# Layer 1 of a two-layer diffusion trunk on Trainium2: 64 of 256 tokens moved from the dense expert products to gathered rows

## Chip, cores and metric

One core of one Trainium2 chip runs the whole program. The metric is device time in microseconds; lower is better. Most executions of a kernel agree within 0.3%.

## What is computed

Two layers over 256 latent and 256 context tokens of width 1024; each is a mixer (attention) and an expert network (PEER) of 16384 experts. Layer 0 needs all 512 tokens, layer 1 only the 256 latents. For each token and each of 8 heads the network takes the best 16 of 16384 experts by product keys, and weights their rows:

```python
q = (xb @ wq).reshape(PEER_TBLOCK, PEER_HEADS, 2, PEER_DQ // 2)
s = jnp.einsum('thpd,pnd->thpn', q, sub_keys).astype(jnp.float32)
sv, si = lax.top_k(s, PEER_TOPK)
...
fv, fp = lax.top_k(cand, PEER_TOPK)
eidx = jnp.take_along_axis(cidx, fp, axis=-1)
g = jax.nn.softmax(fv, axis=-1)
ue = jnp.take(u, eidx, axis=0)
ve = jnp.take(v, eidx, axis=0)
a = jnp.einsum('thkd,td->thk', ue, xb).astype(jnp.float32)
wgt = (jax.nn.gelu(a, approximate=False) * g).astype(xb.dtype)
return jnp.einsum('thk,thkd->td', wgt, ve)
```

So a token has 128 slots (8 heads x 16), each with one row of u and one of v.

## The kernel before, in words

The engines: PE multiplies, ACT casts and evaluates functions, DVE works on elements, POOL (GpSimd) issues gathers, SP issues the other transfers. A float32 matrix is split into a high part, rounded by ACT's cast to the product type (L167), and a low rest that DVE subtracts (L168); a product is then three (L191 to L193: high by high, high by low, low by high). Some products are made in whole float32 instead (L213).

`peer(l, xs, sq, nd)` is the expert network of layer l, with `nd` token blocks of 128 done densely: layer 0 calls it with 3 of 4 blocks, layer 1 with 2 of 2. A dense block multiplies with all 16384 experts, in 128 chunks of 128. For chunk i, `achunk(i)` computes u times the tokens: 24 products (8 parts of the width, three each) whose moving operand has as many columns as there are dense tokens, 384 in layer 0 and 256 in layer 1. ACT applies Gelu into a ring of tiles (L1023). `weight(i)` multiplies the tile with the gate matrix (L1151, zero where the expert is not chosen), and splits it into the tile `w2` (L1152 ACT, L1153 DVE). `split_v(i)` splits v's rows into two `vs` tiles, and `fchunk(i)` multiplies: per dense block two halves of 512 columns, three products each, summed in PSUM over all chunks.

The gate matrix G is built before the loop. `prologue` routes each block (`route`), then `gates` makes 16 groups of 8 tokens per block: DVE and ACT write one-hot operands, PE multiplies them (L954), ACT copies out (L957), and SP writes the stage tile to G in DRAM, read back in the loop as tiles `g` of four chunks, in two buffers (L1139). In the same stretch the first `lag` = 47 calls of `achunk` of layer 1 run, every fifth in whole float32. The main loop then runs j from 0 to 127: load v(j+2), `achunk(j + 47)` while there is one (81 times), `split_v(j+1)`, `weight(j+1)`, `fchunk(j)`. There are four `vs` tiles (two chunks) and two `w2` tiles.

The fourth block of layer 0 goes by gathered rows: its tokens lie on the 128 partitions, and for each of 128 slots POOL issues an indirect DMA of 128 rows of 4 KB into one of five `gr` buffers (L1111), after copying its indices to a small tile (L1105, L1108) whose first copy waits for a `w2` tile and so keeps the pace. DVE multiplies a u row with the token and sums it (L1118); after all u slots, Gelu and gates, it adds each v row with its weight to `acc` (L1123). Layer 1 has none of this.

The order on each engine is set by a scheduler in the language's framework, which moves instructions away from the order in which the code writes them.

Of the kernel before, what the change touches and what calls it, by code (L numbers as in the profile page):

```python
# [10 lines left out]
F = mybir.dt.float32  # L11
# [58 lines left out]
GAT = {"gr": 5, "hn": 1, "ga": 1, "idx": 1, "ix": 3}  # L70
# [5 lines left out]
class Phase:  # L76
    """a pool whose tags have a set number of buffers"""
# [13 lines left out]
class Kernel:  # L91
# [103 lines left out]
    def proj_t(self, key, hh, hl, c=512, **kw):  # L195
        """[128 columns, c tokens] in PSUM"""
# [35 lines left out]
    def ada_mm(self, l, v, half, pool):  # L232
        """half of one modulation vector for both conditions, in rows 0 and 1 of each 32 as four partial sums"""
# [142 lines left out]
    def rope(self, x, p, perm, cos, sin, n):  # L376
        """x [128, n] from p in PSUM, its first 256 columns (the latents) rotated, the rotation after the next one"""
# [59 lines left out]
    def probs1(self, P, S, scale, sink=None, bias=None):  # L437
        """P [128, 2, nk] <- exp of the two heads' scores less their maximum; sums in sm"""
# [31 lines left out]
    def flip(self, x, nk, eng):  # L470
        """[128, 128 nk] -> [128 keys, nk, 128]"""
# [113 lines left out]
    def mixer1(self, xs, sq):  # L585
# [10 lines left out]
        # cq | ckv in natural layout  # L596
# [38 lines left out]
        # kr (replicated), dq, dk transposed  # L635
# [17 lines left out]
        # latent queries, keys and values  # L653
# [124 lines left out]
    def top16(self, V, X, a, b):  # L778
        """sorted top 16 of each a, b as scratch, interleaved over the lists"""
# [12 lines left out]
    def route_scores(self, l, T, nd, hh, hl):  # L792
        """sorted top 16 of each half key for the dense blocks; scores of a further block go to DRAM"""
# [44 lines left out]
    def route(self, sv, al):  # L838
        """experts i, j and gates of one token block; a generator, leaves them in self.rt"""
# [63 lines left out]

    def gates(self, go, ti, G):
        """gate matrix of 128 tokens -> DRAM; a generator"""
# [58 lines left out]
        for n in range(16 + GPIPE):  # L964
            if n < 16:
# [6 lines left out]
    def peer(self, l, xs, sq, nd):  # L972
        """nd dense token blocks; a further block, if any, goes by gathered rows; returns the pieces of f"""
# [3 lines left out]
        TD = nd * 128  # L977
# [9 lines left out]
        rg = Phase(self.tc, "ring%d" % l, {"ring": lag + 2})  # L987
        self.wn = Phase(self.tc, "win%d" % l, W_BUFS)
        routes, sd = self.route_scores(l, T, nd, hh, hl)
        G = self.dp.tile([32, 128, 4 * nd, 4, 32], F, name="G%d" % l)  # L990
# [34 lines left out]
        # routing and gate matrix, with the first products of the main loop in between  # L1025
        def prologue():
            for _ in routes[0]:
                yield RW
            for t in range(nd):
                nxt = routes[t + 1] if t + 1 < nd else None  # L1030
                for n, _ in enumerate(self.gates(self.rt[t], t, G)):
# [3 lines left out]
                if nxt:  # L1035
                    for _ in nxt:
                        yield RW

# [8 lines left out]
        tot = (6 * nd - EARLY[l]) * RW + nd * (32 + 2 * GPIPE)  # L1047
# [14 lines left out]
        mn = Phase(self.tc, "main%d" % l, {**MAIN, **(GAT if T > nd else {})})  # L1062
        acc = None
        if T > nd:
            acc = self.const([128, 1024], name="acc")
            nc.vector.memset(acc, 0.0)
            ga = mn.t("ga", [128, 2, 128])
            idx = mn.t("idx", [128, 128], I32)
            hn = mn.t("hn", [128, 1024])
            for half in range(2):  # L1070
                p = self.ps([128, 4, 128])
                for k in range(4):
                    tt = slice(TD, TD + 128)
                    nc.tensor.matmul(p[:, k, :], hh[:, half * 4 + k, tt], self.identr, start=True, stop=False)
                    nc.tensor.matmul(p[:, k, :], hl[:, half * 4 + k, tt], self.identr, start=False, stop=True)
                nc.scalar.copy(hn[:, half * 512:half * 512 + 512], p.rearrange("p a b -> p (a b)"))
# [21 lines left out]
        def gather(n0, n1, after=None):  # L1098
            """rows of slots n0..n1, not before after is there"""
            n1 = min(n1, 256)  # L1100
# [5 lines left out]
            for a, b in ((n0, min(n1, 128)), (max(n0, 128), n1)):  # L1106
                if a < b:
                    nc.gpsimd.tensor_copy(ix[:, a - n0:b - n0], idx[:, a % 128:a % 128 + b - a])  # L1108
# [351 lines left out]
```

## Time and profile before

| | us |
|---|---|
| median of 3 runs | 2739.52 (2731.03 to 2754.28) |
| span of the profiled execution | 2734.2 |
| PE busy in it | 2610.7 (95%) |
| DVE busy | 1876.3 (69%) |
| ACT busy | 1267.3 (46%) |
| POOL busy | 529.2 (19%) |

The span runs from the first to the last instruction of the execution that the profiler recorded; its own time with what lies around the span is not listed, the runs are timed without the profiler. Busy shares are means over all stages, so each stage is to be read by itself. A product's duration is longer than its distance to the next, since products overlap: rates are read from starts. In the groups, the last figures are the idle time of the engine just before, and what ended most of it.

### The profile page before, as it was taken

The numbers are of one execution on the slowest core, as the hardware profiler recorded it, in microseconds if no ns is written. First come the engines' busy times: TensorE is split into PE (matmuls) and PEld (weight loads), VectorE is DVE, ScalarE is ACT, GpSimd is POOL, SyncE is SP. The second block draws the span as 40 slices with busy tenths as digits, with TensorE's granted clock in tenths as the row PEclk, the third lists the DMA queues.
The fourth block names the chain that finished last, engine by engine and source line by source line (L and its number), as shares of the span: only waits on it lengthen the run. The fifth ranks groups of instructions, "written<-read, shape, count | busy, mean of one in ns | idle before, by whom it ended". The sixth has DMA issues, their size and how long they took to land.

```text
span 2734.2 us, 43073 instructions
## 1 busy us (share of the span) xinstructions
PE 2610.7 (95%) x16265; PEld 2261.8 (83%) x16265; DVE 1876.3 (69%) x3862; ACT 1267.3 (46%) x2201; POOL 529.2 (19%) x534
## 2 busy tenths in 40 slices
PE   7999998989999999999999989998999999999998
PEld 6866787878899999999899767757999899999986
DVE  4267588886977777777777765365997565555455
ACT  3255335997333333333333333343499444444454
POOL 0000000000045555566565530000000000000000
PEclk9999999999999999999999998998999999999999
DMA  7262323977688888888888862453467976565355
GB/s 291 101 216 86 111 88 128 287 235 246 232 313 311 308 315 306 316 299 321 294 309 288 275 225 75 164 195 113 144 215 242 318 267 210 208 211 214 130 193 183
DMA packets 240977, 614.15 MB, mean 225 GB/s; under 512 B 18384, under 2 KB 102608, under 8 KB 240768
## 3 DMA queue, kind: packets, MB, share of 16 engines
q1 hardware_dynamic: 203904, 477.17, 50.6%
q0 software_dynamic: 36864, 134.23, 13.9%
q8 instruction: 127, 2.08, 0.3%
q14 instruction: 82, 0.67, 0.1%
HBM read 558.90 MB, written 52.43 MB: 224 GB/s over the span
## 4 chain that ended last, share of the span: by engine, by line
PE 62%; DVE 6%; DMA 3%; ACT 3%; issue 2%; POOL 1%; SPq 0%; DVEq 0%; POOLq 0%; ACTq 0%
PE p L192 19%; PE p L191 19%; PE p L193 19%; DMA gr<-in_v,ix 1%; PE p L213 1%; PE s L707 1%; PE p L229 1%; DVE ws L168 1%; ACT stage L957 1%; ACT og L940 1%; DVE vs L168 1%; DMA sc<-sd 1%; PE p L954 1%; ACT ws L167 1%; PE p L245 0%
## 5 line engine op out<-in xcount | busy, mean ns | idle before, releaser
L167 ACT CAST ws<-w 128x1024 fp32r<-128x1024 f32 (+1 forms) x327 | 343.0, 1050 | 634.0 <-PE p L192 581.4
L168 DVE TENSOR_TENSOR ws<-w,ws 128x1024 fp32r<-128x1024 f32 (+1 forms) x327 | 397.5, 1216 | 267.7 <-ACT ws L167 267.4
L192 PE MATMUL p<-vs,w 128*128 128x512 f32 x1280 | 502.2, 393 | 7.5 <-DVE vs L168 7.5
L167 ACT CAST vs<-v 128x1024 fp32r<-128x1024 f32 x256 | 269.5, 1053 | 509.5 <-PE p L192 509.5
L191 PE MATMUL p<-vs,w 128*128 128x512 f32 x1280 | 499.6, 391 | 4.4 <-ACT vs L167 4.4
L193 PE MATMUL p<-vs,w 128*128 128x512 f32 x1280 | 501.6, 392 | 0.0
L191 PE MATMUL p<-hh,ws 128*128 128x384 f32 (+2 forms) x1336 | 472.2, 354 | 6.2 <-ACT ws L167 2.9
L193 PE MATMUL p<-hh,ws 128*128 128x384 f32 (+2 forms) x1336 | 466.0, 349 | 1.5 <-DVE ws L168 1.5
L192 PE MATMUL p<-hl,ws 128*128 128x384 f32 (+2 forms) x1336 | 466.6, 349 | 0.0
L168 DVE TENSOR_TENSOR vs<-v,vs 128x1024 fp32r<-128x1024 f32 x256 | 312.8, 1222 | 152.7 <-ACT vs L167 151.0
L191 PE MATMUL p<-hp,ws 128*128 128x256 f32 x1032 | 295.5, 287 | 1.8 <-ACT ws L167 1.1
L193 PE MATMUL p<-hp,ws 128*128 128x256 f32 x1032 | 292.8, 284 | 0.8 <-DVE ws L168 0.8
L192 PE MATMUL p<-hp,ws 128*128 128x256 f32 x1032 | 293.2, 284 | 0.0
L192 PEld LDWEIGHTS p<-vs,w 128*128 128x128 f32 x1280 | 241.3, 189 | 56.5 <-DVE vs L168 11.1
L193 PEld LDWEIGHTS p<-vs,w 128*128 128x128 f32 x1280 | 240.9, 188 | 53.7 <-DVE w L1153 3.0
L191 PEld LDWEIGHTS p<-vs,w 128*128 128x128 f32 x1280 | 241.1, 189 | 50.6 <-ACT vs L167 4.6
L191 PEld LDWEIGHTS p<-hh,ws 128*128 128x128 f32 x1336 | 255.0, 191 | 24.7 <-ACT ws L167 4.3
L192 PEld LDWEIGHTS p<-hl,ws 128*128 128x128 f32 x1336 | 254.6, 191 | 14.9 <-issue 0.5
L193 PEld LDWEIGHTS p<-hh,ws 128*128 128x128 f32 x1336 | 254.5, 190 | 13.1 <-DVE ws L168 2.0
L1123 DVE SCALAR_TENSOR_TENSOR acc<-gr,ga,acc 128x1024 f32<-128x1024 f32 x128 | 164.2, 1283 | 102.3 <-DMA gr<-in_v,ix 101.7
L1118 DVE SCALAR_TENSOR_TENSOR gr<-gr,hn 128x1024 f32<-128x1024 f32 x128 | 156.2, 1224 | 108.5 <-DMA gr<-in_u,ix 102.5
L311 POOL TENSOR_TENSOR rso<-rsm,mhalf 128x1 f32<-128x1 f32 x30 | 20.1, 671 | 1079.4 <-DVE rsm L309 1079.4
(267 smaller groups left out, 4127.6 us busy)
## 6 DMA issues: line engine op xcount, KB each, us to landing
w<-in_uT SPq DMA_DIRECT2D x256, 512.0 KB
v<-in_v SPq DMA_DIRECT2D x256, 512.0 KB
w<-in_ada_w SPq DMA_DIRECT2D x96, 512.0 KB
G<-stage SPq DMA_DIRECT2D x40, 1024.0 KB
g<-G SPq DMA_DIRECT2D x32, 768.0 KB
w<-in_wq SPq DMA_DIRECT2D x32, 512.0 KB
g<-G SPq DMA_DIRECT2D x32, 512.0 KB
w<-in_w_out SPq DMA_DIRECT2D x16, 512.0 KB
```

What stands on the lines that cost most here:

```text
L167: self.nc.scalar.copy(hi, raw)
L168: self.nc.vector.tensor_tensor(lo, raw, hi.bitcast(F), op=OP.subtract)
L191: m(out, lh, rh, start=start, stop=False)
L192: m(out, lh, rl, start=False, stop=False)
L193: m(out, ll, rh, start=False, stop=stop)
L213: self.nc.tensor.matmul(out, w[:, k * 128:(k + 1) * 128], self.h32[:, k, :], start=k == 0, stop=k == 7)
L229: self.nc.tensor.transpose(out, x, self.ck("ident"))
L707: nc.tensor.matmul(S[:, s, :], a[c][h, q], b[c][h, :], start=True, stop=kind == "d", tile_position=(64 * s, 0))
L940: nc.scalar.activation(og_[:, 1, g, :, b], oh[:, 1, g, :, b], AF.Copy, scale=gl[:, k:k + 1])
L954: nc.tensor.matmul(p[:, k, :], oh[:, 0, g, :, b], og_[:, w, g, :, b], start=(w == 0), stop=(w == 1))
L1118: nc.vector.scalar_tensor_tensor(t, t, 1.0, hn, op0=OP.mult, op1=OP.mult, accum_out=ga[:, 0, n:n + 1])
L1123: nc.vector.scalar_tensor_tensor(acc, t, ga[:, 0, n - 128:n - 127], acc, op0=OP.mult, op1=OP.add)
```

## The change

Layer 1 calls `peer(1, xs, sq, 1, 1)`: one dense block of 128 tokens, and the second block is split. Its first 64 tokens stay dense, but their weights' high and low parts lie side by side as one operand of 128 columns, so that two products (with v high, v low) take the place of three; the sum of the two halves of the result is taken at the end by a product with a matrix `fold`. Its other 64 tokens go by gathered rows: each token lies on two partitions, 64 slots on each (`spread` moves the indices and gates there), so that there are 64 gathers of u rows and 64 of v rows, spread over the loop from its first iteration, with six buffers. The u products have 192 columns, the gate tiles 192 tokens, and the gate groups are 16 + 8 in place of 32. The low part of the 64 packed tokens is subtracted on POOL. u and v become one tensor per layer.

```diff
-GAT = {"gr": 5, "hn": 1, "ga": 1, "idx": 1, "ix": 3}
+GAT = {0: {"gr": 5, "hn": 1, "ga": 1, "idx": 1, "ix": 3}, 1: {"gr": 6, "hn": 1, "ix": 3, "pk": 2}}
...
-            self.nc.tensor.matmul(out, w[:, k * 128:(k + 1) * 128], self.h32[:, k, :], start=k == 0, stop=k == 7)
+            self.nc.tensor.matmul(out, w[:, k * 128:(k + 1) * 128], self.h32[:, k, :out.shape[-1]], start=k == 0, stop=k == 7)
...
-        TD = nd * 128
+        GT = 64 if packed else 128
+        GS = 128 * GT // 128
+        TD = T * 128 - GT
+        NP = TD // 32
+        DD = nd * 128
...
-                for n, _ in enumerate(self.gates(self.rt[t], t, G)):
+                if t == nd:
+                    spread(self.rt[t])
+                for n, _ in enumerate(self.gates(self.rt[t], t, G, 16 if t < nd else 8)):
...
+            ii = self.wn.t("rt", [128, 128], I32, name="ii")
+            nc.vector.scalar_tensor_tensor(ii, go[:, 0, :], 128.0, go[:, 1, :], op0=OP.mult, op1=OP.add)
+            for s in range(2):
+                nc.sync.dma_start(idx[64 * s:64 * s + 64, :], ii[64:128, 64 * s:64 * s + 64])
+                nc.sync.dma_start(ga[64 * s:64 * s + 64, 1, :], go[64:128, 2, 64 * s:64 * s + 64])
...
+        if packed:
+            hd = mn.t("gr", [128, 8, 2, GT], name="hd")
+            for s in range(2):
+                nc.gpsimd.tensor_copy(hd[:, :, s, :], self.h32[:, :, tt])
...
+                if packed:
+                    self.transpose(p[:, k, :], hd[:, kk].rearrange("p s t -> p (s t)"))
...
-            nc.scalar.copy(w[:, 0, :], wl)
-            nc.vector.tensor_tensor(w[:, 1, :], wl, w[:, 0, :].bitcast(F), op=OP.subtract)
+            nc.scalar.copy(w[:, :TD], wl)
+            h = w[:, :TD].bitcast(F)
+            if packed:
+                nc.gpsimd.tensor_tensor(w[:, TD:TD + GT], wl[:, DD:], h[:, DD:], op=OP.subtract)
+            nc.vector.tensor_tensor(w[:, 2 * TD - DD:], wl[:, :DD], h[:, :DD], op=OP.subtract)
...
+            if packed:
                 for half in range(2):
                     for i, vh, vl, w in ops:
                         b = slice(half * 512, half * 512 + 512)
-                        self.mm3(fps[t][half], w[:, 0, tt], w[:, 1, tt], vh[:, b], vl[:, b], i == 0, i == NCH - 1)
+                        for m, v in enumerate((vh, vl)):
+                            nc.tensor.matmul(fps[nd][half], w[:, DD:DD + 128], v[:, b], start=i == 0 and m == 0,
+                                             stop=i == NCH - 1 and m == 1)
...
-        NGB = 5
-        lt = late() if T > nd else None
+        NGB = GAT[l]["gr"]
+        first = 0 if packed else LATE
+        lt = None if packed else late()
...
+                pk = mn.t("pk", [128, 512])
+                nc.scalar.copy(pk, fps[nd][half])
+                p = self.ps()
+                for s, x in enumerate((pk, acc[:, half * 512:half * 512 + 512])):
+                    nc.tensor.matmul(p[64 * s:64 * s + 64, :], self.fold, x, start=True, stop=True,
+                                     tile_position=(0, 64 * s))
```

The new lines keep their places a little further down: L168 of before is L169, L1151 is L1181, L1153 is L1186, L1118 is L1148, L1111 is L1141; POOL's subtraction is L1185.

The scheduler gives DVE another order where layer 1's main loop begins. Before, from the splits of the first two chunks of v (vs) to those of the third and the fourth (ws is a split of u, ring<-ring,g the multiply with the gates, w the low part of the weights):

```order
L168 TENSOR_TENSOR vs<-v,vs 128x1024 x2
L1151 TENSOR_TENSOR ring<-ring,g 128x256
L168 TENSOR_TENSOR ws<-w,ws 128x1024
L1151 TENSOR_TENSOR ring<-ring,g 128x256 x2
L168 TENSOR_TENSOR vs<-v,vs 128x1024
L1153 TENSOR_TENSOR w_20847<-ring,w_20847 128x256
```

Now, from the same two splits to that of the third chunk (gr,ga<-gr,hn is the use of a gathered u row):

```order
L169 TENSOR_TENSOR vs<-v,vs 128x1024 x2
L169 TENSOR_TENSOR ws<-w,ws 128x1024
L1181 TENSOR_TENSOR ring<-ring,g 128x192 x4
L169 TENSOR_TENSOR ws<-w,ws 128x1024
L1181 TENSOR_TENSOR ring<-ring,g 128x192 x16
L169 TENSOR_TENSOR ws<-w,ws 128x1024
L1181 TENSOR_TENSOR ring<-ring,g 128x192
L1148 SCALAR_TENSOR_TENSOR gr,ga<-gr,hn 128x1024 x7
L169 TENSOR_TENSOR ws<-w,ws 128x1024
L1148 SCALAR_TENSOR_TENSOR gr,ga<-gr,hn 128x1024
L169 TENSOR_TENSOR vs<-v,vs 128x1024
L1186 TENSOR_TENSOR w_20659<-ring,w_20659 128x128
```

Between the second and the third split of v stood four instructions; now there stand 33: 21 multiplies with the gates of later chunks, four splits of u and eight uses of gathered rows.

POOL had nothing of layer 1's main loop; the row before the end of its list, the factors of the norms, is all that stood there. Now it has this as the loop begins (hd is the copy of the 64 tokens, ix the index tile):

```order
L1096 COPY hd<-h_17511 128x8x64 x2
L1138 COPY ix<-idx 128x6
L1141 DMA gr<-in_u,ix 128x1024 x2
L1185 TENSOR_TENSOR w_20538<-ring,w_20538 128x64
L1141 DMA gr<-in_u,ix 128x1024 x3
L1185 TENSOR_TENSOR w_20596<-ring,w_20596 128x64
L1135 COPY ix<-w_20596 128x1
L1138 COPY ix<-idx 128x2
L1141 DMA gr<-in_u,ix 128x1024 x3
L1185 TENSOR_TENSOR w_20659<-ring,w_20659 128x64
```

Each chunk's subtraction now stands in one list with the index copies and the gathers.

## Rows read from the trace of the kernel before

**Rows 1.** The page's head: the span of the profiled execution.

```profile
span 2734.2 us, 43073 instructions
```

**Rows 2.** Windows (us, each engine's busy us and count, PE clock, DMA share, GB/s).

```profile
736.00:1173.00 437.00, 436.49 (x2205) 396.77 (x2205) 329.57 (x482) 150.84 (x208) 227.25 (x224) 1.00 0.87 311
1950.00:2117.60 167.60, 161.46 (x1462) 154.72 (x1461) 144.62 (x343) 146.06 (x278) 0.00 (x0) 0.99 0.67 211
2117.60:2139.90 22.30, 17.89 (x138) 17.27 (x136) 8.99 (x12) 12.16 (x20) 0.00 (x0) 1.00 1.01 340
2139.90:2591.00 451.10, 451.10 (x2879) 411.38 (x2880) 264.14 (x364) 213.67 (x319) 0.00 (x0) 1.00 0.62 219
2591.00:2718.80 127.80, 127.80 (x567) 105.54 (x566) 72.05 (x93) 62.81 (x93) 0.00 (x0) 1.00 0.57 197
...
2132.00:2144.00 12.00, 7.59 (x41) 6.52 (x40) 7.17 (x12) 5.07 (x8) 0.00 (x0) 0.86 0.98 380
```

**Rows 3.** Timeline of PE in layer 1's loop (start us, us, engine, line, op).

```profile
2301.71 0.28 PE L191 MATMUL p<-hp,ws 128*128 128x256 f32 x1
...
2304.58 0.40 PE L191 MATMUL p<-vs,w 128*128 128x512 f32 x1
...
2307.33 0.28 PE L191 MATMUL p<-hp,ws 128*128 128x256 f32 x1
```

**Rows 4.** Timeline of PE and its weight loads (PEld), layer 0.

```profile
662.05 0.22 PE L1074 MATMUL p<-identr,hh 128*128 128x128 f32 x1
...
662.10 0.28 PE L1075 MATMUL p<-identr,hl 128*128 128x128 f32 x1
662.16 0.19 PEld L1074 LDWEIGHTS p<-identr,hh 128*128 128x128 f32 x1
662.22 0.27 PE L1074 MATMUL p<-identr,hh 128*128 128x128 f32 x1
```

**Rows 5.** Timeline of PE before layer 1's loop.

```profile
2083.18 3.67 PE L213 MATMUL p<-h,w 128*128 128x256 f32 x16
2086.69 2.00 PE L954 MATMUL p<-og,oh 128*128 128x128 f16 x32
2088.73 0.39 PE L191 MATMUL p<-hp,ws 128*128 128x256 f32 x1
```

**Rows 6.** The page's groups: DVE on gathered rows (count, busy us, mean ns, idle).

```profile
L1123 DVE SCALAR_TENSOR_TENSOR acc<-gr,ga,acc 128x1024 f32<-128x1024 f32 x128 | 164.2, 1283 | 102.3 <-DMA gr<-in_v,ix 101.7
L1118 DVE SCALAR_TENSOR_TENSOR gr<-gr,hn 128x1024 f32<-128x1024 f32 x128 | 156.2, 1224 | 108.5 <-DMA gr<-in_u,ix 102.5
```

**Rows 7.** Groups of POOL; last, one line's durations (ns min/median/max).

```profile
L1111 POOL DMA_INDIRECT gr<-in_v,ix x128 | 177.1, 1383 | 45.1 <-POOL ix L1108 22.5 <-issue 21.1 <-DVE ws L168 0.9
...
L1108 POOL COPY ix<-idx 128x3 int32<-128x3 int32 (+3 forms) x111 | 88.3, 796 | 188.1 <-DVE idx L1091 181.5
L1105 POOL COPY ix<-w 128x1 f32<-128x1 f32 x109 | 65.6, 602 | 277.2 <-ACT w L1152 276.4 <-issue 0.3
...
L1105 POOL COPY ix<-w x109: 181/473/2787, 766.0 to 1594.6; 128x1 f32<-128x1 f32 x109
```

**Rows 8.** Timeline of DVE, then of POOL, in layer 0's loop.

```profile
916.06 1.22 DVE L168 TENSOR_TENSOR ws<-w,ws 128x1024 fp32r<-128x1024 f32 x1
...
916.24 1.09 POOL L1108 COPY ix<-idx 128x3 int32<-128x3 int32 x1
```

**Rows 9.** Timeline of DVE and PE as layer 1's loop begins ([idle before <-releaser]).

```profile
2136.49 1.09 DVE L1151 TENSOR_TENSOR ring<-ring,g 128x256 f32<-128x256 f32 x3 [7.98 <-DMA g<-G]
...
2139.90 1.91 PE L191 MATMUL p<-vs,w 128*128 128x512 f32 x4 [4.41 <-ACT vs L167]
```

**Rows 10.** Timeline of ACT, DVE and PE in the loop's tail.

```profile
2651.04 1.05 ACT L167 CAST vs<-v 128x1024 fp32r<-128x1024 f32 x1 [1.36 <-PE p L192]
...
2652.13 1.22 DVE L168 TENSOR_TENSOR vs<-v,vs 128x1024 fp32r<-128x1024 f32 x1 [1.16 <-ACT vs L167]
...
2653.79 0.39 PE L191 MATMUL p<-vs,w 128*128 128x512 f32 x1
```

More of the change, by code (lines that the diff above doesn't have):

```diff
@@ L962, in product @@
                                       stage[:, 64 * c:64 * c + 64, :].rearrange("p (c i) t -> p c (i t)", i=4))
-        for n in range(16 + GPIPE):
-            if n < 16:
+        for n in range(blocks + GPIPE):
+            if n < blocks:
                 build(n)
@@ L970, in gates, with peer @@
             yield
-    def peer(self, l, xs, sq, nd):
+    def peer(self, l, xs, sq, nd, packed):
         nc = self.nc
@@ L986, in peer @@
         self.m.close()
-        rg = Phase(self.tc, "ring%d" % l, {"ring": lag + 2})
+        rg = Phase(self.tc, "ring%d" % l, {"ring": lag + 2, **GIDX[l]})
         self.wn = Phase(self.tc, "win%d" % l, W_BUFS)
-        routes, sd = self.route_scores(l, T, nd, hh, hl)
-        G = self.dp.tile([32, 128, 4 * nd, 4, 32], F, name="G%d" % l)
+        routes, sd = self.route_scores(l, T, nd + packed, hh, hl)
+        G = self.dp.tile([32, 128, NP, 4, 32], F, name="G%d" % l)
         self.rt = []
@@ L1028, in prologue @@
                 yield RW
-            for t in range(nd):
-                nxt = routes[t + 1] if t + 1 < nd else None
-                for n, _ in enumerate(self.gates(self.rt[t], t, G)):
+            for t in range(nd + packed):
+                nxt = routes[t + 1] if t + 1 < nd + packed else None
+                if t == nd:
+                    spread(self.rt[t])
+                for n, _ in enumerate(self.gates(self.rt[t], t, G, 16 if t < nd else 8)):
                     yield 1
@@ L1046, in peer @@
         i = 0
[L1047 removed]
+        tot = (6 * (nd + packed) - EARLY[l]) * RW + nd * (32 + 2 * GPIPE) + packed * (16 + 2 * GPIPE)
         done = 0
@@ L1061, in peer @@
         self.wn.close()
[L1062 to L1076, printed above, removed]
+        mn = Phase(self.tc, "main%d" % l, {**MAIN, **GAT[l]})
+        if self.acc is None:
+            self.acc = self.const([128, 1024], name="acc")
+        acc = self.acc
+        nc.vector.memset(acc, 0.0)
+        if not packed:
+            ga = mn.t("ga", [128, 2, GS])
+            idx = mn.t("idx", [128, GS], I32)
+        hn = mn.t("hn", [128, 1024])
+        tt = slice(TD, TD + GT)
+        if packed:
+            hd = mn.t("gr", [128, 8, 2, GT], name="hd")
+            for s in range(2):
+                nc.gpsimd.tensor_copy(hd[:, :, s, :], self.h32[:, :, tt])
+        for half in range(2):
+            p = self.ps([128, 4, 128])
+            for k in range(4):
+                kk = half * 4 + k
+                if packed:
+                    self.transpose(p[:, k, :], hd[:, kk].rearrange("p s t -> p (s t)"))
+                else:
+                    nc.tensor.matmul(p[:, k, :], hh[:, kk, tt], self.identr, start=True, stop=False)
+                    nc.tensor.matmul(p[:, k, :], hl[:, kk, tt], self.identr, start=False, stop=True)
+            nc.scalar.copy(hn[:, half * 512:half * 512 + 512], p.rearrange("p a b -> p (a b)"))
         def late():
@@ L1181, in peer @@
         weight(0)
+        if packed:
+            gather(0, NGB)
         for j in range(NCH):
@@ L1198, in peer @@
         fchunk([NCH - 2, NCH - 1])
+        if not packed:
+            f = [[acc[:, 0:512], acc[:, 512:1024]]]
+        else:
+            f = []
+            for half in range(2):
+                pk = mn.t("pk", [128, 512])
[4 more added lines that the diff above has]
+                                     tile_position=(0, 64 * s))
+                f.append(p)
+            f = [f]
         mn.close()
         rg.close()
-        return [fps[t] if t < nd else [acc[:, 0:512], acc[:, 512:1024]] for t in range(T)]
+        return fps[:nd] + f
     def residual(self, l, f):
@@ L1264, in run @@
         nc.vector.tensor_copy(self.io2, self.ck("iota")[:, :, None].to_broadcast([128, 128, 2]))
+        self.acc = None
+        self.fold = self.const([128, 64], name="fold")
+        nc.vector.tensor_tensor(self.fold, self.ck("ident")[:, 0:64], self.ck("ident")[:, 64:128], op=OP.add)
         self.identr = self.const([128, 128], R, name="identr")
@@ L1438, in layout @@
     z["uT"] = peer_u.reshape(2, 128, 128, 8, 128).transpose(0, 1, 4, 3, 2)
-    z["u0"] = peer_u[0]
-    z["v"] = peer_v
+    for l in range(2):
+        z["u%d" % l], z["v%d" % l] = peer_u[l], peer_v[l]
     z["fg"] = final_norm_g
```

47 lines of the change are left out of this document (28 added, 19 removed).

## Prediction

> **What bounds the kernel now.** I read the windows first, one row per stage, then the timeline inside a stage for who waits for whom, then the groups by line for durations. Of the 2734.2 us [rows 1] the change reaches the expert block of layer 1. In it TensorE (PE) is busy nearly all the time: 161.5 of 167.6 us from the routing to the last gate product, 17.9 of 22.3 us in the change over to the main loop, 451.1 of 451.1 and 127.8 of 127.8 us in the loop [rows 2]. So the loop is a string of PE products. While u products remain, an iteration costs 24 of them with 256 columns in 2304.58 - 2301.71 = 2.87 us (0.120 each) and 12 v products with 512 columns in 2307.33 - 2304.58 = 2.75 us (0.228 each): 5.62 us [rows 3]. The last 48 iterations are v products alone, 12 x 0.228 = 2.72 us. As a check, 80 x 5.62 + 48 x 2.72 = 580 us, and from the first F at 2139.9 [rows 9] to 2718.8 PE is full in each row of rows 2, 578.9 us. VectorE (DVE) has slack there (264 of 451 us) and GpSimd (POOL) does nothing at all [rows 2].
>
> **The change part by part.** I write A for the 24 u products of a chunk and F for its v products.
>
> *F: 12 products become 10* (six for the dense block, four for high and low side by side): 10 x 0.228 = 2.28 us, 0.45 us less.
>
> *A: 256 columns become 192.* No row has 192. From 0.228 at 512 and 0.120 at 256 the slope is 0.42 ns a column, which gives 0.093. But with 128 columns the products of [rows 4] follow each other at 0.11 (662.10 to 662.22, with a weight load that begins between them at 662.16), while the first pair, whose loads were taken during the wide product before, was 0.05 apart (662.05 to 662.10) [rows 4]. So I read the load as a floor of 0.11, and a narrow product as not slower by itself. I take 0.111: A is 2.66 us, 0.22 less; ends 0.093 and 0.120. "TensorE: Matmul & The Clock Gate" of the Trainium skill, section LDWEIGHTS, says the same against this change: a load takes its columns over 1.2 GHz, estimated at 107 ns, whatever the product's width; by streaming alone A would be 2.23 us and the loop some 35 us shorter than I say.
>
> So on PE alone an iteration would be 4.93 us, then 2.28 us. Whether it gets there hangs on four covers.
>
> *DVE.* It gains 64 u rows (1.22 us) and 64 v rows (1.28 us) [rows 6], 128 uses over 206 half iterations: 1.24 per full iteration, 0.62 in a tail one. Its multiply shrinks from 0.36 (1.09 for three, [rows 9]) to about 0.28 and its subtraction to 0.21. A full iteration has 2 x 1.15 for the splits (1.22 us in rows 8; I take off the overlap of one instruction with the next, which the three multiplies of rows 9 show too), 0.28, 0.21 and 1.24 x 1.18: 4.25 us of 4.93. It fits, with 14% to spare.
>
> *POOL* is new in this loop: a subtraction of 64 columns per chunk, two small index copies and the gathers' descriptors. A gather takes 1.38 plus 0.35 of idle (45.1 us over 128) [rows 7]; 1.24 of them are 2.1 us, the copies 0.60 and 0.80: 3.5 us without the subtraction. No row has that. Its bounds are the shortest and the longest copy of one element, 0.2 and 2.8 [rows 7]. A three element copy lasted 1.09 us because DVE's split, begun 0.18 before it, ended 1.04 after it [rows 8]; so I take 0.35 for the work and 0.65 for the wait, 1.0: 4.5 us of 4.93. The Trainium skill's "SBUF — State Buffer", section "SBUF: two separate sides", has the rule: the port pair of DVE and GpSimd is an exclusive lock, and who starts first holds it for the whole instruction. Rows 8 agree, with 1.09 us. By the rule at its full price every subtraction waits out a whole split, 1.55 in all, and the sum below would be -3; with no lock at all the tail would run at PE's 2.28 and the sum would be -58.
>
> *DMA.* A full iteration loads u and v (0.524 MB each), a quarter of the gate tile (0.098) and 1.24 x 0.524 of gathered rows: 1.80 MB. At 4.93 us that is 365 GB/s. The loop of layer 0 had 311 at a DMA share of 0.87 with PE full, and the change over 380 at 0.98 [rows 2]. So it is just below what was seen, with queueing. With these three near 90% I give a full iteration 5.10 us: 80 x (5.62 - 5.10) = 42 us less; ends 4.93 (55 less) and 5.78 (1.80 MB at 311; 13 more).
>
> *The tail.* Here two buffers of vs and w2 make a chain: ACT's vs cast starts as F(j-1) ends (2651.04), DVE's split follows (2652.13 for 1.22), F(j+1) starts at 2653.79 [rows 10], about 2.75 us after the cast. Today this is in time by some 0.4 us. With F at 2.28 it is not: the packed products come first and need POOL's low part, and POOL must wait until that split ends, 2.3 us after the cast, then 0.35. Period 2.7; in the 62% of iterations with a gather POOL is late by another 0.5 to 1. I take 3.0: 48 x (3.0 - 2.72) = 13 us more; ends 2.28 (21 less) and 3.9 (57 more, POOL's subtraction at 2.0).
>
> *Before the loop.* 33 split A chunks at 24 x 0.009 = 7.1 us; 9 chunks in whole float32 whose 16 products take 0.219 (3.51 / 16, [rows 5]) and in proportion 0.165: 7.6 us; 8 gate groups of 16 products at 0.064 (2.04 / 32): 8.2 us. Together 22.9; with PE at 161.5 of 167.6 I take 20; ends 15 and 23. The last five chunks gain nothing: from the last gate product to the first F PE waits anyway for G to be written and read back (DVE idle 7.98 for it, PE 4.41, [rows 9]), and the copies, transposes and hn lie in that wait. Cost 0; if the copies are late, 3.
>
> *The order at the loop's start* costs. Before, DVE has three multiplies and one ws split between the second and the third vs split. Now it has 21 multiplies, four ws splits and eight uses there: 5.9 + 4.6 + 9.4 = 20 us of work, and the gate tile has two buffers, so each four multiplies wait for a load. PE has F, A, F, A to do meanwhile, 9.9 us. So PE waits 10 us for DVE's work alone; with some 2 us for each of four loads 18, with the 14 multiplies and a use before the next split 22, and with the clock that falls after such a pause (0.86 in the stretch with the 4.41 us pause, [rows 2]) 24. Ends 10 and 32.
>
> *The end.* Four products fold the halves, behind the last F, while DVE works on the first block: 1 us; ends 0 and 3.
>
> Sum: -20 + 24 - 42 + 13 + 1 = -24 us on the profiled 2734.2: 2710. The median of the runs, 2739.5, lies 5.3 above that span (the page gives the span alone, so what lies around it I leave as it is): about 2716.
>
> **Rivals.**
> 1. *The covers hold, PE alone decides.* -20 + 10 - 55 - 21 + 1 = -85: 2655. For it: PE was full in layer 0 beside gathers [rows 2]. Against: three engines at 90%, and the order above.
> 2. *Slower: POOL becomes the bound.* Place: the subtraction between index copies and descriptors. At T us for it an iteration takes 3.5 + T, a tail one 1.9 + T (0.62 of 3.1, plus T). It eats the whole gain from T = 1.6 (tail 3.5, 37 us more instead of 13); at T = 2.0 the sum is -20 + 24 - 10 + 58 + 1 = +53: 2793. For it: copies of one to three elements took 0.6 and 0.8 on average and up to 2.8 [rows 7]. Against: T that high needs a full wait each time, and DVE has gaps.
> 3. *DMA becomes the bound.* At 311 GB/s: +13 in full iterations, 0.95 MB in 3.05 us in the tail +16, -20 + 24 + 1: +34, 2773. For it: no long stretch shows more. Against: 380 over 12 us.
> 4. *The narrow product is dearer*, two passes a column: 0.173, 2870. Against: the 0.05 of [rows 4].
>
> **How the numbers follow.** Forecast 0.52, its own range 2690 to 2745; rival 1 0.22, rival 2 0.13, rival 3 0.08, rival 4 0.05. A difference under 1% (27 us) is about what a measurement of this kernel cannot tell from none. Under 2712 lie rival 1 and 45% of the forecast: 0.45. Over 2767 lie nearly all of rivals 2 and 4 and half of rival 3: 0.21. The rest is 0.34. The range leaves out a tenth below, where all covers hold and the start costs nothing, and a tenth above: 2665 to 2780.
>
> **What would show it.** Starts of u products with 192 columns 0.11 apart; full iterations of 5.0 to 5.2 us and tail ones of 2.7 to 3.2, where PE's waits name POOL's subtraction; one wait of PE of 10 us or more for vs within 30 us of the loop's start; DMA near 350 GB/s. It is wrong if PE waits in the loop for gathers or u loads instead, if the subtraction takes over 1.6 us, or if the start runs through.

## The result, and the profile after

| | before | changed |
|---|---|---|
| median of 4 runs, us | 2739.95 (2731.03 to 2754.28) | 2835.75 (2830.6 to 2847.5) |
| ratio to before (95% interval) | | 1.0345 (1.0317 to 1.0373) |
| span of the profiled execution, us | 2734.2 | 2828.5 |

The changed kernel is slower by 3.45%. The forecast was 2716, with a range from 2665 to 2780. The windows of the changed kernel by stage (columns as in rows 2): routing to the last gate product, the change over to the first F, the first four iterations, the other 76 full ones, the tail, and a piece of the first four.

```profile
1952.00:2107.60 155.60, 141.72 (x1315) 138.83 (x1314) 128.02 (x300) 118.65 (x226) 2.26 (x2) 0.96 0.63 196
2107.60:2135.90 28.30, 19.79 (x149) 19.31 (x146) 10.07 (x16) 13.77 (x23) 8.47 (x11) 0.82 1.02 360
2135.90:2186.30 50.40, 27.12 (x139) 23.38 (x137) 30.95 (x69) 10.31 (x16) 13.66 (x16) 0.70 0.77 265
2186.30:2653.40 467.10, 408.57 (x2586) 361.61 (x2584) 331.43 (x457) 193.74 (x303) 235.56 (x325) 0.95 0.84 287
2653.40:2814.50 161.10, 127.16 (x483) 94.13 (x481) 99.08 (x120) 61.23 (x95) 73.11 (x110) 0.94 0.71 232
2150.00:2170.00 20.00, 10.29 (x36) 8.68 (x37) 17.90 (x35) 1.95 (x3) 10.72 (x10) 0.51 0.67 215
```

Where rows 2 had PE full in every stretch of the loop, it now idles 23 of 50, 59 of 467 and 34 of 161 us. The times by stage, counted between the starts of F products, in us (the last two columns belong to experiments below):

| stage | before | changed | difference | forecast | uses behind | ramp |
|---|---|---|---|---|---|---|
| start of the first F | 2139.9 | 2135.9 | -4.0 | -20 | | |
| first 4 iterations | 24.2 | 50.4 | +26.2 | +22 | 49.3 | 19.9 |
| the other 76 full ones | 427.1 | 467.2 | +40.1 | -40 | 377.0 | 377.0 |
| 48 tail ones | 130.6 | 161.0 | +30.4 | +13 | 134.4 | 132.7 |
| after the last F | 12.4 | 14.0 | +1.6 | +1 | | |

The forecast's 42 for 80 iterations and 24 for the start are shared out here as 40 and 22. The start is as forecast in size; the 76 iterations have the wrong sign. What PE and DVE waited for in these 76 (waits by engine: who for whom, us in total, times, longest):

```profile
PE p L1198 <- DVE vs L169: 55.8, 32, 5.1
PE p L1198 <- POOL w L1185: 2.4, 1, 2.4
...
DVE gr L1148 <- DMA gr<-in_u,ix: 68.0, 32, 6.6
DVE acc L1153 <- DMA gr<-in_v,ix: 65.9, 17, 7.9
```

PE waits for DVE's split of v, DVE waits for gathered rows. DVE is busy 331.4 of these 467.1 us and waits 133.9 for rows, together 465.3: it has hardly any other idle time, so its work and its waits for rows make up the iteration. The timeline shows one such pause, on POOL, DVE, PE, ACT, and then the next gather and its use:

```profile
2235.05 0.97 POOL L1141 DMA_INDIRECT gr<-in_u,ix  x1 [0.27 <-POOL ix L1138]
2236.33 1.90 POOL L1141 DMA_INDIRECT gr<-in_u,ix  x1 [0.30 <-issue]
...
2238.88 1.21 DVE L169 TENSOR_TENSOR vs<-v,vs 128x1024 fp32r<-128x1024 f32 x1
...
2241.43 1.23 DVE L1148 SCALAR_TENSOR_TENSOR gr<-gr,hn 128x1024 f32<-128x1024 f32 x1 [1.13 <-DMA gr<-in_u,ix]
...
2245.28 1.23 DVE L1148 SCALAR_TENSOR_TENSOR gr<-gr,hn 128x1024 f32<-128x1024 f32 x1 [2.62 <-DMA gr<-in_u,ix]
...
2247.83 1.22 DVE L169 TENSOR_TENSOR vs<-v,vs 128x1024 fp32r<-128x1024 f32 x1
...
2249.11 1.65 PE L1198 MATMUL p<-vs,w 128*128 128x512 f32 x3 [3.72 <-DVE vs L169]
...
2252.92 1.04 ACT L168 CAST vs<-v 128x1024 fp32r<-128x1024 f32 x1 [6.59 <-PE p L193]
2253.87 0.35 ACT L1182 CAST w<-ring 128x192 fp32r<-128x192 f32 x1
...
2254.30 1.30 POOL L1185 TENSOR_TENSOR w<-ring,w 128x64 fp32r<-128x64 f32 x1 [8.70 <-ACT w L1182]
...
2257.27 0.98 POOL L1141 DMA_INDIRECT gr<-in_u,ix  x1 [0.27 <-POOL ix L1138]
...
2263.64 1.23 DVE L1148 SCALAR_TENSOR_TENSOR gr<-gr,hn 128x1024 f32<-128x1024 f32 x1 [6.48 <-DMA gr<-in_u,ix]
```

A gather issued at 2235.05 is used at 2241.43, the next, of 2236.33, at 2245.28. Between two splits of v (2238.88 and 2247.83) stand two uses that wait 1.13 and 2.62 us, and PE loses 3.72. Then the pause comes back: PE's late F holds ACT's vs cast (6.59), behind which stands the cast of w, on which POOL's subtraction and the pace of the gathers wait (8.70), so the next row is issued late and DVE waits 6.48 for it.

By the trace's packet records, a use of a u row in layer 1 starts 6.8 us after its gather is issued (median), and the last packet lands at 5.9; in layer 0 it is 7.6 and 6.0. Six buffers are there, but little more than one row is under way when DVE reaches its use. The code writes a use five iterations behind its gather. DVE's list shows it as a place: the last of the 64 u uses stands five splits of v earlier than in the list of the next section, where the uses keep the code's iterations.

The product itself came out as forecast. PE's timeline, at full clock and after a pause (granted clock 0.51 in the last window above):

```profile
2119.78 0.28 PE L193 MATMUL p<-hp,ws 128*128 128x192 f32 x1
2119.90 0.27 PE L194 MATMUL p<-hp,ws 128*128 128x192 f32 x1
2120.01 0.27 PE L192 MATMUL p<-hp,ws 128*128 128x192 f32 x1
...
2153.17 0.41 PE L192 MATMUL p<-hp,ws 128*128 128x192 f32 x1
2153.38 0.41 PE L193 MATMUL p<-hp,ws 128*128 128x192 f32 x1
```

Starts are 0.11 apart at 2.4 GHz and 0.21 at 1.2 GHz, so after a pause that lowers the clock the next products take longer as well.

### The profile page after: what moved, and what is told of

It reads as the page before. It is cut to its first block, busy times and chain, and to the rows that moved or that the text cites. A ratio compares the mean times of both kernels' runs of the same rounds, so it can differ in the third digit from the quotient of the medians.

```text
span 2828.5 us, 43041 instructions
## 1 busy us (share of the span) xinstructions
PE 2574.0 (91%) x15897; PEld 2204.7 (78%) x15897; DVE 1989.0 (70%) x4034; ACT 1231.9 (44%) x2158; POOL 860.7 (30%) x997
## 3 DMA queue, kind: packets, MB, share of 16 engines
q1 hardware_dynamic: 195968, 468.84, 49.3%
## 5 line engine op out<-in xcount | busy, mean ns | idle before, releaser
L168 ACT CAST ws<-w 128x1024 fp32r<-128x1024 f32 (+1 forms) x327 | 342.2, 1047 | 645.4 <-PE p L193 586.0
L168 ACT CAST vs<-v 128x1024 fp32r<-128x1024 f32 x256 | 269.2, 1052 | 602.6 <-PE p L193 572.8
L169 DVE TENSOR_TENSOR ws<-w,ws 128x1024 fp32r<-128x1024 f32 (+1 forms) x327 | 398.1, 1220 | 177.5 <-ACT ws L168 173.2
L193 PE MATMUL p<-vs,w 128*128 128x512 f32 x1024 | 409.0, 400 | 5.2 <-DVE vs L169 5.1
L194 PE MATMUL p<-vs,w 128*128 128x512 f32 x1024 | 409.6, 400 | 0.0
L192 PE MATMUL p<-vs,w 128*128 128x512 f32 x1024 | 404.2, 396 | 0.0
L1153 DVE SCALAR_TENSOR_TENSOR acc<-gr,ga,acc 128x1024 f32<-128x1024 f32 x192 | 246.6, 1285 | 205.3 <-DMA gr<-in_v,ix 196.2
L1148 DVE SCALAR_TENSOR_TENSOR gr<-gr,hn 128x1024 f32<-128x1024 f32 x192 | 233.9, 1223 | 175.7 <-DMA gr<-in_u,ix 173.0
L169 DVE TENSOR_TENSOR vs<-v,vs 128x1024 fp32r<-128x1024 f32 x256 | 313.3, 1224 | 35.8 <-ACT vs L168 35.5
L194 PE MATMUL p<-hp,ws 128*128 128x192 f32 (+1 forms) x1032 | 290.9, 282 | 20.5 <-DVE ws L169 20.5
L192 PE MATMUL p<-hp,ws 128*128 128x192 f32 (+1 forms) x1032 | 290.9, 283 | 9.3 <-ACT ws L168 8.3
L193 PE MATMUL p<-hp,ws 128*128 128x192 f32 (+1 forms) x1032 | 290.0, 281 | 0.0
L1141 POOL DMA_INDIRECT gr<-in_v,ix x192 | 247.3, 1288 | 63.1 <-POOL ix L1138 35.9
L1198 PE MATMUL p<-vs,w 128*128 128x512 f32 x512 | 169.4, 434 | 106.4 <-DVE vs L169 96.5
L1141 POOL DMA_INDIRECT gr<-in_u,ix x192 | 241.0, 1255 | 82.9 <-issue 50.0
L193 PEld LDWEIGHTS p<-vs,w 128*128 128x128 f32 x1024 | 196.7, 192 | 49.6 <-DVE vs L169 9.0
```

Of the source, the lines that this page charges most:

```text
L168: self.nc.scalar.copy(hi, raw)
L169: self.nc.vector.tensor_tensor(lo, raw, hi.bitcast(F), op=OP.subtract)
L192: m(out, lh, rh, start=start, stop=False)
L193: m(out, lh, rl, start=False, stop=False)
L194: m(out, ll, rh, start=False, stop=stop)
L1141: nc.gpsimd.indirect_dma_start(out=gat[n], out_offset=None, in_=A[("u%d" if n < GS else "v%d") % l], in_offset=bass.IndirectOffsetOnAxis(a ...
```

## The experiments

Theory 1: the uses of gathered rows stand in DVE's order right behind their gathers and hold the splits. Theory 2: DMA is the bound. Theory 3: POOL's subtraction is. All kernels below start from the changed one. Layer 1 begins at another time in each execution (its first gate product between 1986.3 and 2013.3 us) though the code before it is the same, so small differences are read from the loop and not from the total.

**Uses behind.** `issue_after` queues what a block issues on an engine behind a given instruction there; no data or wait changes.

```diff
-            nc.vector.tensor_tensor(w[:, 2 * TD - DD:], wl[:, :DD], h[:, :DD], op=OP.subtract)
+            lows[i] = nc.vector.tensor_tensor(w[:, 2 * TD - DD:], wl[:, :DD], h[:, :DD], op=OP.subtract)
...
-                for n in range(nu, n1):
-                    use(n)
+                with self.tc.issue_after(lows[j + 1].ins):
+                    for n in range(nu, n1):
+                        use(n)
```

> Edit: each use of a gathered row (L1148, L1153) is queued on DVE behind the low subtraction of the iteration in which the code writes it; DVE's list then has the same mix, but each use stands five iterations later, so its row has been under way for five iterations and not for one. Theory 1 (in the changed kernel a use stands on DVE right behind its gather, 6.8 us after the issue where the last packet lands at 5.9, and holds the vs split behind it): DVE's waits for gathered rows (172 us from 2185 to 2815) nearly vanish, full iterations go from 6.15 to 5.0-5.1 us and tail ones from 3.35 to 2.5-2.6; the stall of 31 us at the loop's start shrinks by at most 9 (the eight uses). Sum -84 -41 -8: about 2700, 2690 to 2740. Theory 2 (DMA: 1.80 MB per full iteration at the 300 GB/s seen, and 0.95 MB in the tail): full iterations stay at 5.8-6.0, tail ones at 3.1: 2790 to 2820. Theory 3 (POOL's subtraction between copies and descriptors): nothing moves there, 2820 to 2840.

Measured: 2723.21, ratio to before 0.9934 (0.9902 to 0.9965); the edit takes back 112.5 us. Windows by stage (the first four, the 76 and the tail), then two F starts:

```profile
2150.10:2199.50 49.40, 27.57 (x139) 24.09 (x138) 27.66 (x64) 10.30 (x16) 8.57 (x14) 0.69 0.78 271
2199.50:2576.40 376.90, 376.90 (x2586) 346.27 (x2585) 337.11 (x462) 194.04 (x303) 289.25 (x326) 1.00 0.96 356
2576.40:2710.90 134.50, 122.06 (x483) 89.38 (x481) 104.12 (x123) 61.27 (x95) 93.96 (x112) 0.97 0.81 277
```

```profile
2303.67 1.10 PE L1198 MATMUL p<-vs,w 128*128 128x512 f32 x4
2308.63 1.10 PE L1198 MATMUL p<-vs,w 128*128 128x512 f32 x4
```

PE is full for 377 us, an iteration takes 4.96, and DVE's groups show no wait for a row at all (mean ns, then idle):

```profile
L1153 DVE SCALAR_TENSOR_TENSOR acc<-gr,ga,acc 128x1024 f32<-128x1024 f32 x64 | 81.6, 1275 | 0.2
L1148 DVE SCALAR_TENSOR_TENSOR gr<-gr,hn 128x1024 f32<-128x1024 f32 x64 | 76.7, 1213 | 0.0
```

In the changed kernel these two had 104.1 and 68.8 us. The same gathers, uses and subtractions are there, only the order is another: theory 1 holds, 2 and 3 fall for the full iterations. The first four are as slow as in the changed kernel.

**No gathers.** As above, but only the first six rows are gathered.

```diff
-            if n0 >= n1:
+            if n0 >= n1 or (packed and n0 > 0):
...
-            t = gat.pop(n)
+            t = gat[n % 5] if packed else gat.pop(n)
...
-                nc.vector.scalar_tensor_tensor(t, t, 1.0, hn,
+                nc.vector.scalar_tensor_tensor(gat[5] if packed else t, t, 1.0, hn,
```

> Edit: the same, and only the first six rows are gathered; the other 122 uses read those again (so the values of the 64 gathered tokens are left out of the result). DVE's work and order in the loop stay, POOL's index copies and descriptors and 64 MB of gathered rows go. Theory 1: as fast as the kernel with the uses behind, within 15 us: 2690 to 2720, because waiting for rows was the cost and not the transfers. Theory 2 (DMA): 1.15 MB per full iteration fits easily, so this one alone goes to about 2690 and the one with gathers stays 80 us or more above it. Theory 3 (POOL): the subtraction has POOL to itself, about 2690 too, and the one with gathers stays near 2830.

**No uses.** The changed kernel without the uses.

```diff
-                for n in range(nu, n1):
-                    use(n)
+                if not packed:
+                    for n in range(nu, n1):
+                        use(n)
```

> Edit: the changed kernel with its 128 gathers, index copies and pace, but without the uses on DVE (the part of the 64 gathered tokens is left out of the result). DMA and POOL are loaded as before, DVE never waits for a row. Theory 1: the loop's stalls go with the uses: full iterations 5.0-5.1 us, tail ones 2.4-2.5, 2690 to 2720. Theory 2 (DMA): full iterations stay at 5.8-6.0 us, 2780 to 2820. Theory 3 (POOL): stalls on the subtraction stay, 2780 or more.

Measured: 2699.12, ratio 0.9852 (0.9822 to 0.9882), and 2704.33, 0.9866 (0.9835 to 0.9897). All but the first iterations take 4.96 in both, so neither the rows' transfer nor DVE's work sets the full iteration; only the wait of one for the other did. The tails (without gathers, then without uses):

```profile
2556.10:2675.70 119.60, 117.31 (x483) 87.02 (x481) 102.92 (x122) 61.31 (x95) 40.55 (x46) 1.00 0.66 211
```

```profile
2562.70:2690.10 127.40, 118.45 (x483) 86.92 (x481) 71.80 (x95) 61.25 (x95) 77.48 (x112) 1.00 0.84 289
```

With both it was 134.5: the gathers cost the tail some 15 us, of which 8 stay without the uses.

**Order of the multiplies.** As in uses behind, and each multiply with the gates behind the low subtraction of the chunk before.

```diff
+                    st.enter_context(self.tc.issue_after(lows[i - 1].ins))
                 nc.vector.tensor_tensor(wv, wv, gstr[i // 4][:, :, i % 4, :], op=OP.mult)
```

> Edit: uses queued behind as in the first of these runs, and the multiply with the gates of chunk i+1 queued behind the low subtraction of chunk i as well, so that no multiplies of later chunks stand between the second and the third vs split (four splits of ws and two uses are left there in place of 21 multiplies, four splits and eight uses). Theory 1 with the start as predicted: the start stall (31 us over the first four iterations of the changed kernel) falls to under 8, and the rest is as in the first run: 25 to 30 us faster than it, 2665 to 2690. Rival for the start: it is the DMA backlog (queues 102% busy from 2110 to 2140, DVE waits 11.1 us for a gate tile) and not the order; then the wait moves to the same load, and the gain is under 10 us.

Measured: 2717.81, ratio 0.9932 (0.9907 to 0.9957). The start's stall went to nothing: the first four iterations take 4.98 and three times 4.96. So the order was its cause, and the backlog alone is not. But the tail took 163.8 us, 29 more: now each chunk's multiply is due in the tail, where before it had run ahead. PE waits there (L1185 is the cast of w in this kernel, L1201 the packed products, L1188 POOL's subtraction):

```profile
PE p L192 <- ACT w L1185: 20.1, 16, 2.6
PE p L1201 <- POOL w L1188: 11.8, 19, 1.0
```

**Ramp.** The multiply of chunk i behind the low subtraction of chunk 5i/8 - 1.

```diff
-                    st.enter_context(self.tc.issue_after(lows[i - 1].ins))
+                    st.enter_context(self.tc.issue_after(lows[max(5 * i // 8 - 1, 0)].ins))
```

> Edit: uses queued behind as in the first run, and the multiply of chunk i queued behind the low subtraction of chunk 5i/8-1: few multiplies at the start, 1.6 in each full iteration, so that they run ahead as far as in the first run when the tail begins (in the fourth run one multiply per chunk stayed for the tail, whose iterations took 3.4 us against 2.8). Theory: start as in the fourth run (no stall, 4.96 us from the first iteration), tail as in the first (134 us): 397 + 134 us of loop against 426 + 134 in the first run and 397 + 164 in the fourth; about 2690 (2675 to 2705). Rival: at a DMA share of 0.97 and 366 GB/s the gate tiles that are now loaded sooner (0.06 MB more per iteration) do not fit any more; then full iterations take 5.05 to 5.1 and the time is 2695 to 2710.

Measured: 2687.51, ratio 0.9802 (0.9774 to 0.983). Windows of the first four and the 76:

```profile
2145.50:2165.40 19.90, 19.90 (x139) 18.23 (x138) 14.42 (x23) 9.01 (x14) 15.00 (x14) 1.00 1.03 409
2165.40:2542.30 376.90, 376.90 (x2586) 346.29 (x2585) 344.54 (x501) 195.27 (x305) 300.89 (x325) 1.00 0.98 369
```

PE is full at 2.4 GHz in both, beside 369 GB/s at a DMA share of 0.98; the rival of too much DMA falls.

**Ramp alone**, with the uses where the changed kernel has them.

> Edit: the changed kernel with the ramp for the multiplies alone; the uses of gathered rows stay where they stand in it, right behind their gathers. If the two orders cost independently, the start stall (31 us, of which 29 went in the run with the ramp and the uses behind) goes here too and the waits for rows stay: 2805 to 2815, full iterations still about 6.1 us. Rival (seven uses in a row at the start and the gathers, five of which are issued before the first loads of u, make the start as slow by themselves): 2825 to 2836. Second rival (with the multiplies out of the way the scheduler's uses find their rows landed): under 2760.

Measured: 2820.13, ratio 1.029 (1.0255 to 1.0325). This lies between the expected range and the rival's. The loop went from 678.6 to 654.5 us, all of it in its first four iterations (26.5 in place of 50.4). That is still 6.6 us above the 19.9 of the ramp with the uses behind, so the uses cost a part of the start by themselves, as the rival said. PE still waits for the splits in the whole loop:

```profile
PE p L1201 <- DVE vs L169: 91.2, 45, 5.1
```

Each of the two orders costs time without the other. Over the loops of the four kernels (678.6 changed, 654.5 ramp alone, 560.7 uses behind, 529.5 both) the multiplies' order is worth 24 and 31 us, the uses' 118 and 125.

**Two later.** The changed kernel with the uses two iterations later than they stand there, not five (in the tail, which has half as many uses per iteration, six later and not nine).

```diff
-                with self.tc.issue_after(lows[j + 1].ins):
+                with self.tc.issue_after(lows[max(j - 2, 0)].ins):
```

> Edit: the changed kernel with each use queued on DVE two iterations later than it stands there, in place of five. Theory 1 (it is only the time between the issue of a gather and its use, 6.8 us, against 5.9 to its last packet): two more iterations (10 us) are as good as five, full iterations of 4.96, 2710 to 2735. Rival (six rows in flight are needed, or gathers that all start early keep DMA smooth): DVE still waits for rows, full iterations 5.3 to 5.8, 2755 to 2795.

Measured: 2726.25, ratio 0.9944 (0.9923 to 0.9966). The median from issue to use is 9.9 us for u rows and 12.9 for v rows. Most iterations take 4.96; in the loop from the fifth iteration on some rows are still waited for, 59 us on DVE. PE's waits for splits before the tail are down to 7.1 us, and the 76 iterations take 390.3 us, against 377.0 with the uses behind and 467.2 in the changed kernel:

```profile
DVE acc L1153 <- DMA gr<-in_v,ix: 32.5, 10, 5.8
DVE gr L1148 <- DMA gr<-in_u,ix: 26.5, 14, 3.5
...
PE p L1198 <- DVE vs L169: 7.1, 5, 2.3
```

So two iterations give back 77 of the 90 us of the 76 iterations. The rival has a part: DVE still waits for rows, and an iteration takes 5.13 on average. What counts in the main is the time from issue to use, and six rows in flight are hardly needed.

**The tail: dense first, subtraction on DVE, both.** Each with the ramp: the four packed products behind the six dense ones; `nc.vector` for `nc.gpsimd` in the subtraction of the 64 tokens; both.

> Edit: as in the run with the ramp, and in each chunk the six products of the dense block come before the four packed ones, so that POOL's low part is needed 1.4 us later. Theory (the tail is late by POOL's subtraction, for which PE waited 11.7 us in 15 places in the first run): that wait goes, the tail falls from 134 to 120-124 us, 10 to 14 us faster than the ramp run: about 2678. Rival (the tail is the chain vs cast, DVE split, first product of the next chunk but one, whichever block comes first): within 4 us of it.

> Edit: as in the run with the ramp, and the low part of the 64 packed tokens is subtracted on DVE right beside that of the dense ones; POOL keeps only index copies and gathers. Theory (POOL's wait for DVE's split is the tail's cost, and DVE has room for 0.2 us more in a full iteration at 0.90 busy): full iterations stay at 4.96, the tail falls by 8 to 14 us, about 2680. Rival: DVE becomes the bound: full iterations 5.0 to 5.2, 2695 to 2710.

> Edit: the ramp, dense products first, and the packed tokens' low part subtracted on DVE. Theory (what is left of the tail's excess, 129 us and 127 us for the two edits alone against 119.5 without gathers, is POOL's lateness, of which each edit removed a part): 122 to 124 us, about 2679. Rival (the chain from vs cast over DVE's split and the use of a gathered row sets it): 126 to 130 us, no difference to either.

Measured: 2684.4, 0.9792 (0.976 to 0.9824); 2690.9, 0.9812 (0.9778 to 0.9846); 2686.39, 0.9792 (0.9766 to 0.9818). None can be told from the ramp. The tails, 132.7 with the ramp, are 129.3, 126.8 and 130.3. With dense products first PE's wait for POOL (10.9 us with the ramp) is gone, but it waits in another place:

```profile
PE p L192 <- ACT w L1185: 4.1, 5, 1.2
```

With the subtraction on DVE full iterations keep 4.96 (no rival), and the tail falls by 5.9, less than expected. So POOL's subtraction was the last wait there but hardly the limit: the rivals of the first and of the last hold. What the tail loses beside gathers against 119.6 is not settled. The traces have one more candidate, which no run tried alone: with gathers ACT waits in the tail for loads of v, 19.7 us with the ramp and about as long in the run without uses (20.1), without gathers 1.3 (the ramp, then no gathers):

```profile
ACT vs L168 <- DMA v<-in_v: 19.7, 9, 3.0
```

```profile
ACT vs L168 <- DMA v<-in_v: 1.3, 1, 1.3
```

**The change over.** With the ramp and dense first: two chunks' u products written ahead of the first weights, and the casts of w and v on ACT queued behind theirs; then the multiply and the splits of v on DVE as well (the line with `usplit` stands in the second alone).

```diff
+            if packed:
+                achunk(lag)
+                achunk(lag + 1)
+                st.enter_context(self.tc.issue_after(gelu[lag + 1].ins))
+                st.enter_context(self.tc.issue_after(usplit[lag + 1].ins))
             split_v(0)
             weight(0)
```

> Edit: the version with the ramp and the dense products first, and at the loop's start the u products of the first two iterations are written ahead of the first weights, whose casts on ACT (and those of v) are queued behind them. In the changed kernel and all runs so far PE waits 7.6 to 8.1 us before the first v product for a cast of ws (ACT), which stands on ACT behind two casts of w that wait 11 us for the gate matrix to be written and read back. Theory: this is the rest of the transition's price, 28.3 us from the last gate product to the first v product against 22.5 before; with four casts of ws moved ahead, the wait of 7.8 us and the half clock behind it (24 products at 0.21 in place of 0.11, 2.4 us) go: some 8 us faster than the run with the dense products first, about 2676. Rival: the loads of u are as late as the gate tiles (DMA share 1.02 there), then ACT waits for them and the gain is under 3 us.

> Edit: as in the run with ACT's order at the loop's start, and DVE's multiply and v splits of the first two chunks are queued behind the u splits of chunks 47 and 48 as well. There the wait of 7.8 us for ACT's cast of ws had become one of 4.3 us for DVE's split of ws, which stood behind a multiply that waits 9.9 us for a gate tile, and 2.4 us for the first cast of w. Theory: with that out of the way the transition's wait goes but for what exceeds two chunks of u products (5.3 us), 4 to 8 us faster than the run with the dense products first: 2676 to 2680. Rival: PE has then no more u products than those two chunks and waits for the gate tile itself, within 3 us: it is the write and read of G that sets this wait, as before the change.

Measured: 2683.73, 0.9788 (0.9762 to 0.9815), and 2687.74, 0.9811 (0.9783 to 0.984): no gain. The wait moved each time. In the first DVE's splits of ws stand behind a multiply that waits 9.95 us for the gate tile. In the second PE waits for the first cast of w on ACT, but the gate tile isn't what holds it: the multiply ran at 2123.77, and the cast stands on ACT behind a cast of ws that waits 5.85 us for a load of u (below first the first run, on DVE, then the second, on DVE, ACT and PE):

```profile
2140.74 0.36 DVE L1186 TENSOR_TENSOR ring<-ring,g 128x192 f32<-128x192 f32 x1 [9.95 <-DMA g<-G]
```

```profile
2123.77 0.36 DVE L1186 TENSOR_TENSOR ring<-ring,g 128x192 f32<-128x192 f32 x1 [7.21 <-DMA g<-G]
...
2130.20 1.04 ACT L168 CAST ws<-w 128x1024 fp32r<-128x1024 f32 x1 [5.85 <-DMA w<-in_uT]
...
2132.71 1.22 PE L192 MATMUL p<-vs,w 128*128 128x512 f32 x2 [6.89 <-ACT w L1187]
```

So the rival of the second, that PE would then wait for the gate tile, holds in the time and not in the cause: what PE waits for there is what the rival of the first named, a late load of u. Whether another order on ACT would shorten this stage stays open.

The ramp with dense products first is faster than both kernels: 2684.4, 2.1% under before (1.8 to 2.4). The other five kernels with both orders can't be told from it (ratios of 0.979 to 0.981).

## Why the prediction was wrong

**Full iterations (-40 forecast for the 76 behind the start, +40 measured).** The step that failed is "4.25 us of 4.93. It fits, with 14% to spare". It counted a use as 1.18 us of work and put its wait for the row at nothing. DVE's work came out nearly as forecast, 4.36 us an iteration (331.4 over 76). The wait was 1.76 (133.9 us over 76), together 6.12 of the 6.15 that an iteration took, and with the uses behind it went to nothing and the iteration to 4.96.

The wait stood in the rows: [rows 6] have 108.5 and 102.3 us of idle before 256 uses, 0.82 each. At 1.24 uses that is 1.0 us, and DVE at 5.27 us would have been the bound on paper. That alone would not have given the sign: 5.27 is still a gain of 27 us over the 76. In layer 0 a use waited 0.82 beside a PE with 8.3 us of products an iteration (the first product of F starts at 901.60 and the next one's at 909.91), which hid it; in layer 1, where PE needs 4.96, the 95 uses of the 76 iterations waited 1.41 each. How far a use stood from its gather could be counted from the list, and I read that list for the start alone. Why the wait grew is read from the timeline above, the pause that comes back over ACT and POOL; no run tried that way alone. On PE the same 90 us (467.1 against 376.9) show as 58.5 of idle and 31.7 of longer products, at a granted clock of 0.95 in place of 1.00.

**What of it was right.** The products: 24 at 0.111 and 10 at 0.228, 4.93 forecast, 4.96 measured as soon as the order let PE run. With 192 columns they start 0.11 apart like those with 128 [rows 4]. The Trainium skill's "TensorE: Matmul & The Clock Gate", section LDWEIGHTS, by which a load of 128 columns takes an estimated 107 ns, agrees. DMA at 365 GB/s: 356 over the 377 us with the uses behind, and PE full beside it. Here my caution was wrong: 5.10 was to pay for three engines near 90%, and PE paid nothing with DVE at 0.89, POOL at 0.77 and DMA at 0.96. POOL's subtraction, 1.0 forecast, takes 0.77 there in the changed kernel and 0.93 with the uses behind:

```profile
L1185 POOL TENSOR_TENSOR w<-ring,w 128x64 fp32r<-128x64 f32 x77 | 59.6, 774 | 211.2 <-ACT w L1182 210.3 <-issue 0.7
```

```profile
L1185 POOL TENSOR_TENSOR w<-ring,w 128x64 fp32r<-128x64 f32 x77 | 71.6, 930 | 19.2 <-ACT w L1182 18.2
L1138 POOL COPY ix<-idx 128x1 int32<-128x1 int32 (+1 forms) x76 | 81.5, 1072 | 4.7
```

**The tail (+13 forecast, +30 measured).** The same wait: DVE stood 37.9 us for v rows there.

```profile
DVE acc L1153 <- DMA gr<-in_v,ix: 37.9, 16, 5.8
```

Without it the tail is +3.8, so the chain of casts and splits was dearer on paper (2.7 and more) than on the chip (2.49 without gathers, 119.6 over 48).

**The start (+22 forecast, +26 measured).** The cause was right: multiplies of later chunks, each four behind a load. That the size was right too is in part luck. The sum had 8 us of waits for the four loads, where DVE waited 21.2:

```profile
DVE ring L1181 <- DMA g<-G: 21.2, 8, 11.1
```

And it had 9.4 us of uses. With six of the eight moved away and 15 more multiplies in their place the start took 49.3, no less; with the eight and one multiply, in the run with the ramp alone, it took 26.5, against 19.9 with the ramp and two uses.

**Before the loop (-20 forecast, -4).** The work fell nearly as computed: PE's busy time from 161.5 [rows 2] to 141.7 us, 19.7 where the sum had 22.9. But the stage fell by 12 alone, since PE now waits, twice for long, for splits that stand behind the routing on DVE, and 6 more went in the change over, 28.3 us in place of 22.3, and the stage began 2 us later. "I take 20" took PE's busy share for a bound that would stay.

```profile
1966.73 0.53 PE L194 MATMUL p<-hp,ws 128*128 128x192 f32 x1 [4.77 <-DVE ws L169]
...
2000.23 0.53 PE L194 MATMUL p<-hp,ws 128*128 128x192 f32 x1 [3.55 <-DVE ws L169]
```

**The rivals.** 2793 for a slower outcome through POOL had the sign and not the place. Rival 1, PE alone (2655), is what the full iterations do once the order is mended; the tail and the time before the loop keep 2684 above it. The sentence that named the failure was the last one: PE waits in the loop for gathers, by way of DVE's splits.

## What to carry to other kernels

An instruction that waits for a transfer costs its engine the wait too, and everything queued behind it: take work plus idle from its row before asking whether it fits, and where the iterations are to get shorter, don't count on that idle staying as small (0.82 us a use became 1.41 here). Where work moves to an engine with little slack, count in the order how far each consumer stands from the issue of its transfer, in iterations of the new length; buffers alone don't keep it far. An order that lets work run ahead is of use where slack ends (the tail) and of harm where its input is still under way (the start), so it is worth a ramp.

## What the runs showed of the hardware

PE kept its full rate at 2.4 GHz for 377 us beside 369 GB/s of DMA at a share of 0.98 and DVE at 0.91 (the ramp's window); the longest such stretch of before had 311 [rows 2]. An index copy of one or two elements on POOL took 1.07 us on average with the uses behind, where DVE is busy 337 of 377 us, and in the changed kernel 0.47 with DVE at 331 of 467:

```profile
L1138 POOL COPY ix<-idx 128x1 int32<-128x1 int32 (+1 forms) x76 | 35.8, 471 | 4.7
```
